# Two more load tiles that later hold the split weight parts, loads issued when their tile is free, and slices and list steps in another order

## The chip, the cores and the metric

The kernel runs on one core of a Trainium2 chip. The metric is the device time of one execution in microseconds (us). Before the change three runs took 1670.32, 1674.1 and 1680.08 us; the median is 1674.1.

## The reference: what is computed

One decoder layer on 1024 rows of 1024 columns (T = D = 1024), all in float32. Cut to what matters here:

```python
x = x + token_mixer(rmsnorm(x))          # ends with (g_a * y_a + g_b * y_b) @ w_o
h = rmsnorm(x)
# every row picks one of 4 groups, then two of the 8 experts in it
for each row t and each of its two experts e, with weight g:
    a, b = h[t] @ w_gate[e], h[t] @ w_up[e]         # 1024 -> 512
    out[t] += g * ((silu(a) * b) @ w_down[e])       # 512 -> 1024
x = x + out
x = x + sigmoid(rmsnorm(x) @ w_pg) * (p @ w_pp)
return rmsnorm(x)
```

There are 32 experts; the weights of one are 6 MB, so the experts' stage reads some 200 MB.

## The kernel before: how the work is staged and ordered

TensorE, ScalarE, VectorE and SP run their instructions in the order in which the program writes them from the w_o stage on. A wait of one instruction therefore holds all that is written behind it on its engine. GpSimd's order is left to the scheduler.

**The w_o stage** (818 to 962 us of the profile). There are eight tiles of 128 rows. A tile is 48 matmuls at L423, issued as ticks; `later` sets other work between the ticks of the next tile. When a tile's product is done, `rows_done` (L456) adds x, stores x2 (L502), and calls the functions in `on_rows`, which load weights for the experts. Then, in the ticks of the next tile: at tick 8 the transposes (L108) and `h2_store` (L513: VectorE computes h at L515 into the only h2 buffer, SP stores it at L516); at tick 18 the router's matmuls (L521) and `route_top`, which ends with the mask a at L550; at tick 33 `route_rank`, whose first matmul (L593) reads a, and which scatters two numbers per row into a table (L604). The last tile goes through `last_rows` (L470) instead.

**Weight tiles.** An expert's weights are six chunks of 1 MB (gate, up, gate, up, down, down). `load` (L664) issues one chunk on SP's queue into the next tile of the list `free`, and each load waits until the load five before it has landed. The list has 17 tiles of 8 KB per partition. The first is c0; a0 to a7 and b0 to b7 are tiles that hold the w_o stage's left operand M, so a load into one of them waits until TensorE has read it. `release` appends a tile to the list when its slot is done.

**The entry to the experts** (962 to 986 us). The last routing, the counts of rows per expert, the order of the experts in 32 slots, the index loads (L741 to L743), the first gathers (L701) and the copies of the transposed rows (L799).

**The experts' loop** (L1199, 986 to 1560 us). The string SLOTS gives each of the 32 slots a form: 32 rows (L), 64 (N), 64 + 32 (S), 128 (M), 128 + 32 (X), twice 128 (B), and one with twice 128, then 64, then 32 (A). A block of 128 rows is a wide block. For it the weights are split into a high and a low part so that three fast matmuls replace one (L843); narrow blocks multiply directly (L902, L929). The slots with wide blocks are 9 (B), 11 (X), 14 (M), 16 (A), 20 (B) and 25 (M), and each comes behind a narrow unit. A wide unit has 24 parts of 128x512: 16 for gate and up, 8 for down. A part is split by ScalarE (L97) and then by VectorE (L98), into one of four buffers (PARTS = 4, tiles wph and wpl). `Parts.get(n)` splits on until part n + 3 and hands out part n.

The loop runs one unit ahead: the second half of gate and up of unit u (k = 4 to 7), `act` (silu and product, L906 and L907), the first three k of unit u + 1, `hpose` (transposes and the copy at L916), the fourth k, the down products of u (L929), the stores of y (L940), the transposes of unit u + 2 (L797, L799). On some slots `p_step` adds work of the last stage (L1144). If an expert has more rows than its slot, the rest goes to an overflow list; its four steps on VectorE (`sizes`, L984 to L1023) were written in front of `start(u + 1)` at slots 20, 21, 22 and 23.

**The tail** (1560 to 1675 us) adds the experts' results and computes the last gate and norm.

Of the kernel before, what the change touches and what calls it, by code (L numbers as in the profile page):

```python
# [11 lines left out]
F32R = mybir.dt.float32r  # L12
# [11 lines left out]
NT = 8  # L24
# [14 lines left out]
AHEAD = 5  # L39
PASSES = ((0, 0), (0, 1), (1, 0))  # L40
PARTS = 4
SIZES = (20, 21, 22, 23)


A0, A1, A2, B1, B2, B3 = range(6)
# [14 lines left out]
UNITS = [(s, blocks) for s, k in enumerate(SLOTS) for blocks in KINDS[k]]  # L60
# [5 lines left out]
def layer_kernel(ctx: ExitStack, tc: tile.TileContext, A, out, dbg=None):  # L66
# [70 lines left out]
    big = ctx.enter_context(tc.tile_pool(name="big", bufs=1))  # L137
# [36 lines left out]
    with tc.tile_pool(name="s0", bufs=1, side="right") as s0:  # L174
# [5 lines left out]
        xs, first = [], []  # L180
        for tb in range(NT):
            if tb == 4:
                first = [wchunk(w_in, (4 - i) * D, load_only=True) for i in range(2)]
# [45 lines left out]
    with tc.tile_pool(name="s1", bufs=2) as s1:  # L229
        for cb in range(8):  # L230
# [4 lines left out]
            u = s1.tile([128, KB - 1 + T], F32, name="u")  # L235
# [174 lines left out]
    mpw = ctx.enter_context(tc.tile_pool(name="mpw", bufs=1))  # L410
# [23 lines left out]
    on_rows, last = {}, []  # L434
# [203 lines left out]
    tiles = {}  # L638

    def tile_of(name, dt=F32):  # L640

        if tiles.get(name, (None, None))[1] is not dt:
            tiles[name] = ((mpw if name[0] == "c" else big).tile([128, 2048], dt, name=name), dt)
        return tiles[name][0]

    XP = (mybir.EngineType.SP,)
    ORDER = list(range(6 * NE + 4))

    free = ["c0"] + [f"a{i}" for i in range(7)] + [f"b{i}" for i in range(8)] + ["a7"]
    held, loads = {}, []  # L650

    def chunk_src(c, e):
# [15 lines left out]
    def load(n=1, after=None, last=6 * NE):  # L668

        for _ in range(n):  # L670
            if not free or not ORDER or ORDER[0] >= last:
                return
            q = ORDER.pop(0)
            c, s = q % 6, q // 6
            if s not in ids:
                ids[s] = nc.values_load(slots[:, 1, s:s + 1], engines=XP, min_val=0, max_val=NE - 1)
            held[q] = free.pop(0)
            ld = load_raw(tile_of(held[q]), chunk_src(c, ids[s]), 4 if c < 4 and s < NE else 2)
            if after is None and len(loads) >= AHEAD:
                after = loads[-AHEAD]  # L680
            if after is not None:
                tc.add_manual_dep(ld.ins, after.ins.name,
                                  mybir.DependencyInfo(mybir.DependencyClass.Sync, mybir.DependencyReason.DATA),
                                  reason="few loads under way at once, for the gathers' sake")
                after = None
            loads.append(ld)
# [18 lines left out]
    n = []  # L705
# [10 lines left out]
    first = []  # L716


    for i in range(NT):
        on_rows[i] = [lambda i=i: load(0 if i == NT - 1 else 1 if i else 3)]  # L720

    def x_in(tb):
        if tb < NT:
# [47 lines left out]
    nb = mp.tile([1, 1, NE], F32, name="nb")  # L771
    cums = [mp.tile([1, NE], F32, name=f"cum{i}") for i in range(2)]
    mp.tile([128, 280], F32, name="padm")
    ysc, freeb, nxt = [], ["p0", "p1", "p2", "p3", "p4"], {"xg": 0, "y": 0, "hid": 0}

    def xtile(dt=F32):

# [2 lines left out]
    def turn(what):  # L780
        nxt[what] += 1
        return nxt[what] - 1
# [26 lines left out]
    class Parts:  # L809
# [8 lines left out]
            n -= 16  # L818
            return wpart(self.q + 4 + n // 4)[:, n // 2 % 2, n % 2 * 512:(n % 2 + 1) * 512]

        def get(self, n):
            while self.at < min(n + PARTS, 24):
                h, l = (mp.tile([128, 512], F32R, name=i, bufs=PARTS) for i in ("wph", "wpl"))
                split(h, l, self.raw(self.at))
                self.parts[self.at] = h, l
                self.at += 1
            return self.parts.pop(n)

    class Wide:
# [15 lines left out]
        def gate_up(self, k, j, w):  # L845
            self.mm(self.b[j], [self.x[:, a, k] for a in range(2)], w, k == 0, k == KT - 1)
# [128 lines left out]
    def sizes(step):  # L975

        if step in (1, 2):
            s = xtile()[0:1]
            le, eq = (s[:, i * NOV * NE:(i + 1) * NOV * NE].rearrange("p (i s) -> p i s", i=NOV) for i in range(2))
        (sizes0, sizes1, sizes2, sizes3)[step](*((le, eq) if step in (1, 2) else ()))  # L980
# [46 lines left out]
    def gathers(u):  # L1027

        if u >= len(UNITS):
            return  # L1030
        blocks[u] = []
        e, bs = UNITS[u]
        for r, b in bs:
            xg = XG[turn("xg") % 3]
            if u >= FIXED:
                if r < 128 and ROWS[e] == r:
                    by_few(r, on(n[e], E.Pool), lambda r: gather(xg[:r], places(e, r, b)))
                else:
                    gather(xg[:r], places(e, r, b))
            blocks[u].append([r, xg, None, places(e, r, b), 6 * e])  # L1040
# [18 lines left out]
    def start(u):  # L1059
        if u < len(UNITS):  # L1060
            for i, (r, xg, xt, ix, q) in enumerate(blocks[u]):
                blocks[u][i] = Wide(xt, ix, q) if r == 128 else Rows(r, *xt, ix, q)
            parts[u] = Parts(blocks[u][0].q)

    parts = {}

    def wide(u):
        return [b for b in blocks[u] if b.r == 128], [b for b in blocks[u] if b.r < 128]

    def gate_up(u, ks):  # L1070
        if u < len(UNITS):
            ws, ns = wide(u)
            for k in ks:
                for j in range(2 if ws else 0):
                    w = parts[u].get(2 * k + j)
                    for b in ws:
                        b.gate_up(k, j, w)
                for b in ns:
                    b.gate_up(k)

    def down(u):
        ws, ns = wide(u)
        for b in ns:
            b.down()
        for n in range(8 if ws else 0):
            w = parts[u].get(16 + n)
            for b in ws:
                b.down(n // 2, n % 2, w)

# [109 lines left out]
    for u, (e, _) in enumerate(UNITS):  # L1199
        first, last = (UNITS[u + i][0] != e if 0 <= u + i < len(UNITS) else True for i in (-1, 1))  # L1200
        if first and e + 4 < NE:
            sizes_load(e + 4)
        if first and e == NE - 4:
            nov = nc.values_load(ovi[0:1, 2 * NOV:], engines=(E.PE, E.Activation, E.DVE, E.SP), min_val=0, max_val=NOV)
        gathers(u + 3)
        if u:
            gate_up(u, range(4, 8))
        if last:
            for c in range(4):
                release(6 * e + c)  # L1210
            load(4)
        for b in blocks[u]:
            b.act()
        if first and e in SIZES:
            sizes(SIZES.index(e))
        start(u + 1)
        gate_up(u + 1, range(3))
        for i, b in enumerate(blocks[u]):
            b.hpose()
            if i == 0:  # L1220
                gate_up(u + 1, (3,))
        down(u)
        for b in blocks[u]:
            b.store()
        poses(u + 2)
        if last:
            release(6 * e + 4)
            release(6 * e + 5)
            p_step(e - PROJ)
            p_release(e - PROJ)  # L1230
            if e == NE - 3:
                tails = [tile_of("c2")]
                nc.sync.dma_start(x3_of(0), x2_dram[:128, :])
            load(6)
        if e == NE - 2:
            load(2, last=6 * NE + 4)
# [188 lines left out]
```

## Time and profile before

| | |
|---|---|
| profiled execution | 1677.25 us |
| its span, first to last instruction | 1675.5 us |
| mean granted clock of TensorE | 0.971 |
| TensorE busy | 1545.8 us (92%) |
| VectorE busy | 912.6 us (54%) |
| ScalarE busy | 448.1 us (27%) |
| GpSimd busy | 171.2 us (10%) |
| HBM traffic over the span | 202 GB/s |

The profile is one execution, so its rows belong to 1677.25 us and not to the median of 1674.1. A timeline row reads: start, duration, engine, line, operation, output<-inputs, shapes, count, and in brackets how long the engine was idle ahead of it and what ended that. In the names below PE is TensorE, DVE is VectorE, ACT is ScalarE, POOL is GpSimd, SP is SyncE; SPq rows are DMA issues.

### The profile page before, as it was taken

Reading aid. Unit: us, or ns where it says so; the run is one execution under the profiler, and the core shown is the slowest. Engines: PE = TensorE matmul, PEld = TensorE weight load, DVE = VectorE, ACT = ScalarE, POOL = GpSimd, SP = SyncE. Lnnn points to the kernel's source line nnn. Section 1 sums busy time; section 2 is a strip of 40 time slices with the busy share of each in tenths; the row PEclk is TensorE's granted clock in tenths of the full one; section 3 lists DMA queues with packets and bytes.
Section 4 is the critical chain, followed back from the end, with each engine's and each line's share of the span. In section 5 each row is a group of like instructions: output and inputs, shape, how many; then the busy total and the mean of one; then the engine's idle time right before and its main releaser. Section 6 shows DMA issues by size and latency. Waiting matters only on the chain. (4 is left out here: it accounts for less than half of the span.)

```text
span 1675.5 us, 21390 instructions
## 1 busy us (share of the span) xinstructions
PE 1545.8 (92%) x8328; PEld 1116.4 (67%) x8328; DVE 912.6 (54%) x1266; ACT 448.1 (27%) x695; POOL 171.2 (10%) x318
## 2 busy tenths in 40 slices
PE   6999999999999999999988758999999897889798
PEld 4888888888888888888766623346466462443586
DVE  4899999999972523514533322135463343331575
ACT  4222121112211314622411101024353230220443
POOL 2300000000000001000011111111111101110131
PEclk9999999999999999999999969999999998998999
DMA  5222112211144523444444679999995997899741
GB/s 167 61 64 63 47 54 63 63 55 51 59 142 135 162 89 125 139 138 151 154 173 128 234 279 364 407 409 407 399 405 206 378 369 284 320 372 412 297 164 51
DMA packets 190674, 336.81 MB, mean 201 GB/s; under 512 B 10182, under 2 KB 85022, under 8 KB 190560
## 3 DMA queue, kind: packets, MB, share of 16 engines
q1 hardware_dynamic: 174080, 284.13, 47.1%
q0 software_dynamic: 10576, 29.96, 4.9%
q10 hardware_dynamic: 5904, 21.24, 3.9%
q8 instruction: 67, 1.10, 0.3%
q14 instruction: 47, 0.39, 0.1%
HBM read 302.67 MB, written 35.11 MB: 202 GB/s over the span
## 5 line engine op out<-in xcount | busy, mean ns | idle before, releaser
L164 PE MATMUL mm<-a,wh 128*128 128x512 f32 x1792 | 555.9, 391 | 0.9 <-ACT a L215 0.9
L164 PEld LDWEIGHTS mm<-a,wh 128*128 128x128 f32 x1792 | 336.9, 188 | 70.9 <-ACT a L215 1.5
L164 PE MATMUL mm<-a,wl 128*128 128x512 f32 x896 | 349.3, 390 | 0.0
L256 DVE SCALAR_TENSOR_TENSOR acc<-u,cw,acc 128x1024 f32<-128x1024 f32 x240 | 307.9, 1283 | 7.9 <-ACT acc L239 1.9
L97 ACT ACTIVATE wh<-wraw 128x1024 fp32r<-128x1024 f32 x72 | 76.4, 1061 | 494.7 <-PE mm L164 423.1
L164 PEld LDWEIGHTS mm<-a,wl 128*128 128x128 f32 x896 | 168.5, 188 | 34.7
L164 PE MATMUL mm<-b,wh 128*128 128x512 f32 x512 | 157.5, 389 | 0.0
L843 PE MATMUL p<-wph,xt 128*128 128x512 f32 x432 | 145.1, 405 | 9.3 <-ACT wph L97 9.1
L98 DVE TENSOR_TENSOR wl<-wraw,wh 128x1024 fp32r<-128x1024 f32 x72 | 87.7, 1219 | 72.6 <-ACT wh L97 72.5
L902 PE MATMUL p<-b,xt 128*32 128x256 f32 (+1 forms) x896 | 117.6, 451 | 3.6 <-DMA b<-in_w_exp_up_dram 3.4
L164 PEld LDWEIGHTS mm<-b,wh 128*128 128x128 f32 x512 | 96.1, 188 | 20.0
L843 PEld LDWEIGHTS p<-wph,xt 128*128 128x128 f32 x432 | 82.0, 191 | 37.4 <-ACT wph L97 13.6
L423 PE MATMUL mm<-b,a 128*128 128x512 f32 x384 | 100.6, 412 | 1.4 <-DVE b L98 1.3
L164 PE MATMUL mm<-b,wl 128*128 128x512 f32 x256 | 99.6, 389 | 0.0
L902 PE MATMUL p<-a,xt 128*32 128x256 f32 (+1 forms) x624 | 93.8, 467 | 6.2 <-DMA a<-in_w_exp_gate_dram 3.8
L843 PE MATMUL p<-wpl,xt 128*128 128x512 f32 x216 | 86.1, 399 | 2.1 <-DVE wpl L98 2.1
L940 DVE COPY ys<-p 32x256 f32<-32x256 f32 (+1 forms) x51 | 25.0, 491 | 115.1 <-ACT ys L940 114.7
L423 PEld LDWEIGHTS mm<-b,a 128*128 128x128 f32 x384 | 72.3, 195 | 17.3 <-DVE b L98 2.6
L902 PEld LDWEIGHTS p<-b,xt 128*32 128x32 f32 (+1 forms) x896 | 36.3, 118 | 65.3 <-issue 47.5
L98 DVE TENSOR_TENSOR wpl<-a,wph 128x512 fp32r<-128x512 f32 x88 | 58.9, 687 | 29.1 <-ACT wph L97 28.8
L940 ACT COPY ys<-p 32x256 f32<-32x256 f32 (+1 forms) x51 | 21.3, 417 | 188.5 <-PE p L929 175.7
L97 ACT ACTIVATE wph<-a 128x512 fp32r<-128x512 f32 x88 | 54.5, 629 | 40.6 <-PE p L843 18.8
(333 smaller groups left out, 1667.0 us busy)
## 6 DMA issues: line engine op xcount, KB each, us to landing
a<-in_w_exp_up_dram SPq DMA_DIRECT2D x31, 1024.0 KB, 12.7
a<-in_w_exp_down_dram SPq DMA_DIRECT2D x31, 1024.0 KB, 13.6
b<-in_w_exp_gate_dram SPq DMA_DIRECT2D x30, 1024.0 KB, 15.3
b<-in_w_exp_down_dram SPq DMA_DIRECT2D x30, 1024.0 KB, 13.0
b<-in_w_exp_up_dram SPq DMA_DIRECT2D x29, 1024.0 KB, 12.6
wraw<-in_w_in_dram SPq DMA_DIRECT2D x56, 512.0 KB, 3.7
a<-in_w_exp_gate_dram SPq DMA_DIRECT2D x28, 1024.0 KB, 12.5
ut<-u_dram ACTq DMA_DIRECT2D x24, 512.0 KB, 4.0
```

Of the source, the lines that this page charges most:

```text
L97: nc.scalar.activation(h, src, AF.Copy)
L98: nc.vector.tensor_tensor(l, src, h.bitcast(F32), op=OP.subtract)
L164: nc.tensor.matmul(ps[:, hf], w[wi][:, k], act[ai][k][:, hf * 512:(hf + 1) * 512], start=(k == 0 and i == 0), stop=(k == KT - 1 and i == 2))
L256: nc.vector.scalar_tensor_tensor(acc, u[:, t:t + T], cw[:, cb, t:t + 1], acc, op0=OP.mult, op1=OP.add)
L423: nc.tensor.matmul(ps[-1][:, hf], act(a, k), w(b, k)[:, hf * 512:(hf + 1) * 512], start=(k == 0 and i == 0), stop=(k == nk - 1 and i == 2))
L843: nc.tensor.matmul(o, x[a], w[b], start=first and i == 0, stop=last and i == 2)
L902: nc.tensor.matmul(self.gu[j][p:p + r], self.x[:, k], w[:, i:i + self.gu[0].shape[1]], start=(k == 0), stop=(k == KT - 1))
L940: (nc.scalar.copy if c < len(self.d) // 2 else nc.vector.tensor_copy)(self.y[:, c * n:(c + 1) * n], d)
```

## The change

1. The list of free tiles gets two more, d0 and d1, behind c0. They take loads until chunk 42 (RETIRE, the first of slot 7); from there on they leave the list. The parts of the wide units are then slices of them: four slices of 512 columns of d0 hold the high parts, four of d1 the low ones. The buffers wph and wpl, of the same size together, are gone.
2. `rows_done` of the first tile loads four chunks in place of three, so each later tile's load takes the M tile that has just been multiplied, in place of the next one.
3. `start(u + 1)` stands ahead of the second half of unit u, and where u is narrow and u + 1 wide, `ahead` splits four parts there. `gate_up` gets a limit on how far parts are split: 7 in the first three k, 9 in the fourth.
4. The four steps of the overflow list stand behind `hpose`, at slots 18, 19, 21 and 22.

```diff
-SIZES = (20, 21, 22, 23)
+RETIRE = 42
+SIZES = (18, 19, 21, 22)
...
-            tiles[name] = ((mpw if name[0] == "c" else big).tile([128, 2048], dt, name=name), dt)
+            tiles[name] = ((mpw if name[0] in "cd" else big).tile([128, 2048], dt, name=name), dt)
...
-    free = ["c0"] + [f"a{i}" for i in range(7)] + [f"b{i}" for i in range(8)] + ["a7"]
+    free = ["c0", "d0", "d1"] + [f"a{i}" for i in range(7)] + [f"b{i}" for i in range(8)] + ["a7"]
...
         for _ in range(n):
+            if free and ORDER and free[0][0] == "d" and ORDER[0] >= RETIRE:
+                free.pop(0)
...
-        on_rows[i] = [lambda i=i: load(0 if i == NT - 1 else 1 if i else 3)]
+        on_rows[i] = [lambda i=i: load(0 if i == NT - 1 else 1 if i else 4)]
...
-        def get(self, n):
-            while self.at < min(n + PARTS, 24):
-                h, l = (mp.tile([128, 512], F32R, name=i, bufs=PARTS) for i in ("wph", "wpl"))
+        def ahead(self, n):
+            while self.at < min(n, 24):
+                i = turn("part") % PARTS
+                h, l = (tile_of(t, F32R)[:, i * 512:(i + 1) * 512] for t in ("d0", "d1"))
                 split(h, l, self.raw(self.at))
                 self.parts[self.at] = h, l
                 self.at += 1
+
+        def get(self, n, limit):
+            self.ahead(min(n + PARTS, limit))
             return self.parts.pop(n)
...
+    def ahead(u, n):
+        if u < len(UNITS) and wide(u)[0]:
+            parts[u].ahead(n)
+
-    def gate_up(u, ks):
+    def gate_up(u, ks, limit=24):
...
-                    w = parts[u].get(2 * k + j)
+                    w = parts[u].get(2 * k + j, limit)
...
         gathers(u + 3)
+        start(u + 1)
+        if blocks[u][0].r < 128:
+            ahead(u + 1, PARTS)
         if u:
             gate_up(u, range(4, 8))
...
-        if first and e in SIZES:
-            sizes(SIZES.index(e))
-        start(u + 1)
-        gate_up(u + 1, range(3))
+        gate_up(u + 1, range(3), 7)
         for i, b in enumerate(blocks[u]):
             b.hpose()
             if i == 0:
-                gate_up(u + 1, (3,))
+                gate_up(u + 1, (3,), 9)
+        if first and e in SIZES:
+            sizes(SIZES.index(e))
         down(u)
```

Three places of the instruction order show it. The first is SP's queue in the w_o stage, from the end of the first tile's product on; numbers tell the tiles of a name apart, a0 to a2 are M tiles, x2 and h2 are the rows and their norm. Before:

```order
L502 DMA x2_dram_66<-x2_5279 128x1024
L664 DMA c0_5341<-in_w_exp_gate_dram 128x4x512
L664 DMA a0_5343<-in_w_exp_up_dram 128x4x512
L664 DMA a1_5345<-in_w_exp_gate_dram 128x4x512
L725 DMA x2_5347<-in_x_dram 128x1024
L516 DMA h2_dram_67<-h2_5369 128x1024
L502 DMA x2_dram_66<-x2_5281 128x1024
L664 DMA a2_5483<-in_w_exp_up_dram 128x4x512
L725 DMA x2_5485<-in_x_dram 128x1024
L516 DMA h2_dram_67<-h2_5507 128x1024
```

And now:

```order
L504 DMA x2_dram_66<-x2_5279 128x1024
L666 DMA c0_5341<-in_w_exp_gate_dram 128x4x512
L666 DMA d0_5343<-in_w_exp_up_dram 128x4x512
L666 DMA d1_5345<-in_w_exp_gate_dram 128x4x512
L666 DMA a0_5347<-in_w_exp_up_dram 128x4x512
L729 DMA x2_5349<-in_x_dram 128x1024
L518 DMA h2_dram_67<-h2_5371 128x1024
L504 DMA x2_dram_66<-x2_5281 128x1024
L666 DMA a1_5485<-in_w_exp_down_dram 128x2x1024
L729 DMA x2_5487<-in_x_dram 128x1024
L518 DMA h2_dram_67<-h2_5509 128x1024
```

Ahead of the first store of h the last load went into a1, which the second tile still reads; it now goes into a0, which the first tile has read. The same holds one tile further on (a2 before, a1 now).

The second place is VectorE between slot 10 (narrow) and slot 11 (wide and narrow): L98, now L100, is the split of a part, L907, now L915, slot 10's product, L916, now L924, the copy that its down product reads, L940, now L948, its store. Before:

```order
L907 TENSOR_TENSOR hid_6444<-p_7823,hid_6444 64x256
L98 TENSOR_TENSOR wpl<-b_6454,wph 128x512
L98 TENSOR_TENSOR wpl<-a_6456,wph 128x512
...
L98 TENSOR_TENSOR wpl<-c_5341,wph 128x512
L916 COPY xt<-h 128x128
L98 TENSOR_TENSOR wpl<-a_5343,wph 128x512
L98 TENSOR_TENSOR wpl<-c_5341,wph 128x512
L960 UNCONDITIONAL_BRANCH
L940 COPY ys<-p_8108 32x256 x2
L799 COPY xt<-x_8141 128x512
L960 UNCONDITIONAL_BRANCH
L98 TENSOR_TENSOR wpl<-a_5343,wph 128x512
```

And now:

```order
L100 TENSOR_TENSOR d_7550<-b_6286,d_7549 128x512
L915 TENSOR_TENSOR hid_6446<-p_7703,hid_6446 64x256
L100 TENSOR_TENSOR d_7550<-b_6249,d_7549 128x512
L100 TENSOR_TENSOR d_7550<-b_6286,d_7549 128x512
L100 TENSOR_TENSOR d_7550<-b_6249,d_7549 128x512
L924 COPY xt<-h 128x128
L100 TENSOR_TENSOR d_7550<-b_6286,d_7549 128x512
L100 TENSOR_TENSOR d_7550<-b_6346,d_7549 128x512
L968 UNCONDITIONAL_BRANCH
L948 COPY ys<-p_8038 32x256 x2
L803 COPY xt<-x_8071 128x512
```

Four splits have moved ahead of slot 10's product; three stand between the product and the copy, where nine stood, and two between the copy and the store of y, as before, so that nine of the 24 parts are split ahead of that store in place of eleven.

The third place is GpSimd at the entry to the experts: L604, now L606, is a scatter of the last tile's routing, L701, now L705, the first gather of rows. Before:

```order
L489 TENSOR_TENSOR rs<-rs,mhalf 128x1
L604 DMA table<-pay,dst 32768x2 x2
L701 DMA c_5276<-h_dram,idx_82 64x1024
L708 TENSOR_LOAD slots
L708 ISA x2
```

And now:

```order
L491 TENSOR_TENSOR rs<-rs,mhalf 128x1
L705 DMA c_5276<-h_dram,idx_82 64x1024
L606 DMA table<-pay,dst 32768x2 x2
L712 TENSOR_LOAD slots
L712 ISA x2
```

The gather now stands ahead of the last two scatters.

More of the change, by code (lines that the diff above doesn't have):

```diff
@@ L773, in layer_kernel @@
     mp.tile([128, 280], F32, name="padm")
-    ysc, freeb, nxt = [], ["p0", "p1", "p2", "p3", "p4"], {"xg": 0, "y": 0, "hid": 0}
+    ysc, freeb, nxt = [], ["p0", "p1", "p2", "p3", "p4"], {"xg": 0, "y": 0, "hid": 0, "part": 0}
     def xtile(dt=F32):
@@ L1085, in down @@
         for n in range(8 if ws else 0):
-            w = parts[u].get(16 + n)
+            w = parts[u].get(16 + n, 24)
             for b in ws:
```

## The prediction

> **What bounds the kernel now.** I read the page's slices first, then the list of waits, then the timelines of the stages that the change touches. Each digit of the slices is a tenth of 41.9 us.
>
> ```profile
> PE   6999999999999999999988758999999897889798
> DMA  5222112211144523444444679999995997899741
> ```
>
> TensorE is busy nearly everywhere, so a gain has to come from stretches in which it waits. The low slices 21 to 24 are the w_o stage and the entry to the experts; from slice 25 on transfers are near their limit as well. The waits, with total, count and longest one, show a ring of three in the w_o stage:
>
> ```profile
> PE tp L593 <- DVE a L550: 25.4, 7, 4.8
> DVE h L515 <- DMA h_dram<-h: 49.9, 6, 9.5
> SPq L664 <- PE mm L423: 102.6, 9, 18.3
> ```
>
> Read from below: SP stands 102.6 us at a weight load whose tile is still being multiplied; the store of h queued behind it is late; VectorE cannot overwrite the one h buffer (49.9 us); the routing behind that is late, and TensorE waits for its mask a (25.4 us). SP and VectorE rows of the first two tiles show one turn:
>
> ```profile
> 847.42 0.37 SPq L664 DMA_DIRECT2D a<-in_w_exp_gate_dram  x1
> ...
> 848.44 0.37 SPq L516 DMA_DIRECT2D h_dram<-h  x1
> ```
>
> ```profile
> 836.73 1.28 DVE L515 SCALAR_TENSOR_TENSOR h<-x,rs,gf 128x1024 f32<-128x1024 f32 x1 [2.25 <-POOL rs L103]
> ...
> 856.72 1.28 DVE L515 SCALAR_TENSOR_TENSOR h<-x,rs,gf 128x1024 f32<-128x1024 f32 x1 [8.07 <-DMA h_dram<-h]
> ```
>
> h of tile 0 is ready at 836.73 + 1.28 = 838.0, its store goes out 10.4 us later, right behind the load at 847.42, and VectorE waits 8.07 us for it.
>
> **Term 1, the w_o loads.** TensorE's rows there (start, duration, what it waited for):
>
> ```profile
> 834.54 1.09 PE L108 MATMUL tp<-ident,x 128*128 128x128 f32 x8 [0.67 <-DVE x L458]
> ...
> 848.83 1.04 PE L108 MATMUL tp<-ident,x 128*128 128x128 f32 x8
> ...
> 879.15 3.73 PE L423 MATMUL mm<-b,a 128*128 128x512 f32 x9
> ...
> 915.38 2.29 PE L423 MATMUL mm<-b,a 128*128 128x512 f32 x9
> ...
> 934.57 3.77 PE L423 MATMUL mm<-b,a 128*128 128x512 f32 x9
> ...
> 941.78 1.04 PE L108 MATMUL tp<-ident,x 128*128 128x128 f32 x8
> ...
> 967.99 0.18 PE L593 MATMUL tp<-a,tri 128*128 128x32 bf16 x1 [3.60 <-DVE a L550]
> ```
>
> A tile whose predecessor's store is not yet needed takes 848.83 - 834.54 = 14.29 us; the next five take 941.78 - 848.83 = 92.95 instead of 71.45, that is 21.5 too many. Of the 25.4 us of waits the last, 3.60, is the last tile's own routing with no matmuls left to cover it; it stays. The other six make 21.8. Two of them left the clock at half for nine matmuls (3.73 and 3.77 against 2.29): 2.9 more. Every load now takes a tile that is free when it is issued, so the store goes out when h is ready. Removed: 21.8 + 2.9 = 24.7. What comes late next: four loads stand together behind row 0. At 2.6 us each (term 3) they and 1.5 MB of x, x2 and h, ahead of or behind them, need some 14 us from 835, so h of tile 0 lands at about 850 to 851; VectorE wants the buffer at 836.73 + 14.29 = 851.0, and later tiles have one load each in 14.29 us. I take **-25**, with ends -28 and -21.
>
> **Term 2, the entry to the experts.** GpSimd's rows, and ScalarE's that TensorE's first expert matmul waits for:
>
> ```profile
> 970.39 1.04 POOL L604 DMA_INDIRECT table<-pay,dst  x1 [6.47 <-DVE sm L557]
> 971.74 0.96 POOL L604 DMA_INDIRECT table<-pay,dst  x1 [0.30 <-issue]
> 973.00 1.02 POOL L701 DMA_INDIRECT c<-h_dram,idx  x1 [0.30 <-issue]
> ```
>
> ```profile
> 984.45 0.59 ACT L799 COPY xt<-x 128x512 f32<-128x512 f32 x1 [12.17 <-DMA x_dram<-x]
> ```
>
> The first gather now stands ahead of the last two scatters. SP's next load, and the index loads and the x2 store behind it, wait for that gather, which starts 973.00 - 970.39 = 2.6 us earlier; the index loads also need the scatters, which start 1.3 us later. Between -2.6 and +1.3; I take **-1**.
>
> **Term 3, two more chunks loaded ahead.** Waits of TensorE for weights in the first slots, the rate of the full stretch, and SP later on:
>
> ```profile
> 1026.40 1.09 PE L902 MATMUL p<-b,xt 128*64 128x512 f32 x1 [2.49 <-DMA b<-in_w_exp_up_dram]
> ...
> 1044.18 4.80 PE L902 MATMUL p<-b,xt 128*64 128x512 f32 x34 [0.90 <-DMA b<-in_w_exp_up_dram]
> ```
>
> ```profile
> 1100.00:1200.00 100.00, 93.11 (x596) 57.34 (x596) 50.46 (x83) 42.06 (x74) 13.39 (x14) 1.00 1.04 407
> ```
>
> ```profile
> 1261.24 33.00 SPq L664 DMA_DIRECT2D b<-in_w_exp_down_dram  x2
> ```
>
> At 407 GB/s (last column) a chunk of 1.05 MB takes 2.6 us, so two chunks are a lead of some 5 us: more than the 2.49 + 0.90 = 3.4 us waited. I take **-3.4** (0 to -5). At 1261 SP's two loads span 33 us, as it waits for a free tile: by there transfers have run ahead of the work, and dropping the two tiles at slot 7 costs no supply.
>
> **Term 4, parts split ahead.** From the page's groups (busy, mean ns, idle before, releaser) and around slot 20:
>
> ```profile
> L843 PE MATMUL p<-wph,xt 128*128 128x512 f32 x432 | 145.1, 405 | 9.3 <-ACT wph L97 9.1
> ...
> L843 PE MATMUL p<-wpl,xt 128*128 128x512 f32 x216 | 86.1, 399 | 2.1 <-DVE wpl L98 2.1
> ```
>
> ```profile
> 1331.21 0.50 PE L843 MATMUL p<-wph,xt 128*128 128x512 f32 x1 [1.56 <-ACT wph L97]
> ...
> 1333.91 0.50 PE L843 MATMUL p<-wph,xt 128*128 128x512 f32 x1 [0.56 <-ACT wph L97]
> ```
>
> ```profile
> 1333.22 2.19 ACT L97 ACTIVATE wph<-a 128x512 fp32r<-128x512 f32 x4 [2.07 <-DMA a<-in_w_exp_up_dram]
> ```
>
> The 11.4 us stand at the six starts of wide units, where TensorE arrives before the first parts are split. With four parts split before the narrow unit's second half, they are ready. Not so at slot 20: there ScalarE itself waits 2.07 us for the chunk, so 1.56 + 0.56 = 2.1 remain. **-9.3** (-5 to -12).
>
> **Term 5, fewer parts ready in second halves.** Only part 8 is now ready when a wide unit goes on, where 8, 9 and 10 were; part 9's split stands behind the stores of y and the copy of the next x. Slot 11, and the price of a split:
>
> ```profile
> 1175.63 0.50 PE L843 MATMUL p<-wph,xt 128*128 128x512 f32 x1
> ```
>
> ```profile
> 1175.92 0.85 DVE L940 COPY ys<-p 32x256 f32<-32x256 f32 x2 [2.45 <-ACT ys L940]
> 1176.80 0.69 DVE L799 COPY xt<-x 128x512 f32<-128x512 f32 x1
> ```
>
> ```profile
> L98 DVE TENSOR_TENSOR wpl<-a,wph 128x512 fp32r<-128x512 f32 x88 | 58.9, 687 | 29.1 <-ACT wph L97 28.8
> ...
> L97 ACT ACTIVATE wph<-a 128x512 fp32r<-128x512 f32 x88 | 54.5, 629 | 40.6 <-PE p L843 18.8
> ```
>
> Part 8 feeds three matmuls of 0.4 us, until 1176.8; VectorE is free of the copy at 1177.5 and has part 9 at 1178.2: a new wait of 1.4. Six units like it would cost 8.4; units with two blocks have twice the matmuls as cover and 0.2 left over. I take 1.4 for slot 11, 2.4 for the three other units with one wide block and 0.5 for the two with two: **+4.3** (0 to +9).
>
> **Term 6, the overflow list's steps.** Waits at slots 21 and 22, and the same work undisturbed:
>
> ```profile
> 1396.53 3.68 PE L929 MATMUL p<-b,xt 128*64 128x512 f32 x8 [4.11 <-DVE xt L916]
> ...
> 1404.75 5.40 PE L1144 MATMUL x<-b,b 128*128 128x512 f32 x8 [1.30 <-DVE xt L799]
> ...
> 1418.96 3.61 PE L929 MATMUL p<-a,xt 128*32 128x256 f32 x32 [4.82 <-DVE xt L916]
> ...
> 1440.75 3.70 PE L1144 MATMUL x<-b,b 128*128 128x512 f32 x8 [1.51 <-DVE xt L98]
> ```
>
> ```profile
> 1050.88 3.65 PE L929 MATMUL p<-b,xt 128*64 128x512 f32 x16
> ...
> 1189.81 1.93 PE L929 MATMUL p<-a,xt 128*32 128x256 f32 x32 [0.38 <-DVE xt L916]
> ```
>
> VectorE does a list step of four to six us ahead of the copy that the down product needs; behind that copy the steps run beside the product (3.65 us) and only its end, some 1.1 us each at slots 19 and 21, delays the y stores and the next copies. So -4.11 - 4.82 + 2.2 = -6.7. The clock was at half after these waits: the second product took 3.61 instead of 1.93, and eight matmuls of the first took 3.68, as long as sixteen undisturbed ones (3.65). I take -1.7 - 1.8. **-10.2** (-5 to -14). The matmuls of the projection at 1404.75 also ran at half (5.40 against 3.70), after a wait of only 1.30; as that wait stays, I return nothing for them.
> [...]
>
> **The sum.** -25 - 1 - 3.4 - 9.3 + 4.3 - 10.2 = -44.6. The profiled execution took 1677.25 us, 1675.5 of them span; minus 44.6 that is 1632.65. It lies 3.15 above the median of the three runs, 1674.1, which gives 1629.5. As two small gains are left out (half clock in the last tile and at slot 14, for which I have quoted no row), I say **1628**. About 0.5%, 8.4 us, is what a measurement of this kernel can tell from no change.
>
> **The rivals.** A, *transfers are the bound* from the experts' entry on: terms 4 to 6 give nothing, as TensorE then waits for weights instead. 1674.1 - 29.4 = 1644.7. For it: the 407 GB/s. Against it: SP's long wait for a tile at 1261 and TensorE's 93% in that window. Chance 0.09.
> B, *the four loads hold the queue*: h's store lies behind 4 MB on SP's queue; if it is late by the 10 us of those loads and each later load is again ahead of its store, term 1 goes: 1628 + 25 = 1653. Against it: 851 and 851.0 meet in tile 1, and later tiles have 2.6 us of load per 14.29. Chance 0.08.
> [...] No run here shows four loads ahead of a store.
> C, *slower*: the four parts are slices of two tiles. Were every split to wait for all readers of its tile, each of 6 x 24 = 144 parts would show its 0.63 + 0.69 = 1.32 us, 190 us in all: 1818. It decides from 44.6 / 144 = 0.31 us a part. Against it: y's halves are slices of one tile too, and copies into one go on beside a scatter of the other; the wait in 1175.92 is for ScalarE alone. Chance 0.03.
> D, *nothing moves*: the loads still wait for matmuls, as new free tiles only shift names, and the rest cancels: 1674. Against it: the order of loads shown with the change names tiles already read. Chance 0.03.
>
> **How the numbers follow.** My forecast has 0.77. Its terms' ends, not all at once, make 1612 to 1648, and A lies inside: 0.77 x 0.92 + 0.09 is about 0.8. Faster by over 0.5% are forecast, A and B: 0.94; within it D: 0.03; slower C: 0.03.
>
> **What would show it.** Right: no wait of SP's loads for matmuls of L423, one wait of about 3.6 left at the rank matmul, tiles of 14.3 us, no waits of 4 us at the down products, short new waits at part 9. Wrong: waits for h's store remaining (B), waits for weights at wide starts (A), a split per 1.3 us with TensorE idle (C).

## The result, and the profile after

The changed kernel took 1631.77 us, the median of four runs (1628.60 to 1638.78), beside 1675.49 us for the kernel before: a ratio of 0.9746, with a 95% interval of 0.970 to 0.979. Beside the experiments, in two more sittings that the record puts on one chip, the ratio was 0.968 (0.9655 to 0.9706) and 0.974 (0.9714 to 0.977). These two intervals do not touch, so ratios of different sittings can differ by 0.6% with nothing changed. The forecast was 1628 in a range of 1612 to 1648, with a chance of 0.94 for faster. The profiled execution took 1638.78 us, its span is 1637.0: 38.5 us less than the profiled one before, where the sum said 44.6. It was the slowest of its four; the two later traces of the same kernel, on the chip of those sittings, have spans of 1631.0 and 1632.4, 44.5 and 43.1 us less.

The slices of the page after, to be set against the two rows of before:

```profile
PE   6999999999999999999989968999999888988898
DMA  5221122112225443534385689999996989999641
```

There is one low slice at the entry to the experts now, number 24, and the ones of the w_o stage are filled. The list of waits, with the ring of three in it:

```profile
PE tp L595 <- DVE a L552: 5.8, 2, 3.6
...
DVE h L517 <- DMA h_dram<-h: 6.8, 1, 6.8
...
SPq L666 <- PE mm L425: 4.3, 3, 3.7
```

SP's 102.6 us at the loads are 4.3, VectorE's 49.9 us for the h buffer are one wait of 6.8, and TensorE's 25.4 us are 5.8 in two waits. TensorE's rows show where the two are:

```profile
849.46 1.04 PE L110 MATMUL tp<-ident,x 128*128 128x128 f32 x8
...
860.15 0.19 PE L595 MATMUL tp<-a,tri 128*128 128x32 bf16 x1 [2.16 <-DVE a L552]
...
865.99 1.03 PE L110 MATMUL tp<-ident,x 128*128 128x128 f32 x8
...
874.37 0.19 PE L595 MATMUL tp<-a,tri 128*128 128x32 bf16 x1
...
880.19 1.04 PE L110 MATMUL tp<-ident,x 128*128 128x128 f32 x8
...
922.89 1.04 PE L110 MATMUL tp<-ident,x 128*128 128x128 f32 x8
...
943.66 0.18 PE L595 MATMUL tp<-a,tri 128*128 128x32 bf16 x1 [3.60 <-DVE a L552]
```

From 865.99 on a tile takes 14.2 us (865.99 to 880.19, and 56.90 for the four up to 922.89). Only the second tile, behind the burst of four loads, waited 2.16 us, and the last kept its 3.60.

Both traces have 8328 matmuls in the same order, so the start of one matmul in the trace after can be set against its start before. How far the changed kernel is ahead shows term by term where the time came from:

| TensorE's instruction | before | after | after less before | term, and its step |
|---|---|---|---|---|
| transposes behind w_o tile 0 | 834.54 | 835.17 | +0.63 | |
| last tile's rank matmul | 967.99 | 943.66 | -24.33 | 1: -25.0 |
| first expert matmul | 985.09 | 958.48 | -26.61 | 2: -2.3 |
| slot 6's down product | 1050.88 | 1022.61 | -28.27 | 3: -1.7 |
| start of slot 20 (B) | 1331.21 | 1301.14 | -30.07 | 4 and 5: -1.8 |
| transposes in slot 20 | 1350.55 | 1325.12 | -25.43 | 6: +4.6 |
| slot 21's down product | 1396.53 | 1366.78 | -29.75 | 6: -4.3 |
| slot 22's down product | 1418.96 | 1382.94 | -36.02 | 6: -6.3 |
| a projection step | 1440.75 | 1403.03 | -37.72 | 6: -1.7 |
| start of slot 25 (M) | 1449.28 | 1410.24 | -39.04 | 4: -1.3 |
| end of the span | 1675.5 | 1637.0 | -38.5 | |

The two later traces give -25.7 and -25.5 for the first step, -2.5 and -2.1 for the second, -3.5 and -3.2 for the third and -4.4 and -2.2 for the fourth, so a step of a few us in one trace is good to some two us.

One row is of the wrong sign: behind slot 19 the changed kernel loses 4.6 us. TensorE before:

```profile
1350.55 1.84 PE L108 MATMUL x<-ident,a 128*128 128x128 f32 x8 [1.49 <-DVE xt L799]
```

And after, with VectorE ahead of it:

```profile
1318.61 0.70 PE L801 MATMUL x<-ident,xg 64*128 64x64 f32 x8
1325.12 1.97 PE L110 MATMUL x<-ident,b 128*128 128x128 f32 x8 [5.80 <-DVE xt L803]
```

```profile
1312.19 0.42 DVE L924 COPY xt<-h 128x256 f32<-128x256 f32 x1 [3.11 <-PE h L923]
...
1318.73 1.15 DVE L1009 TENSOR_TENSOR xt<-cum,iota_s 1x960 f32<-1x960 f32 x1 [4.91 <-PE p L937]
...
1323.65 0.69 DVE L948 COPY ys<-p 64x512 f32<-64x512 f32 x1
1324.37 0.69 DVE L803 COPY xt<-x 128x512 f32<-128x512 f32 x1
```

The list step (L1009 and four more up to 1323.6) should have run beside the down product, from 1313.8 on, when VectorE was free. It waited 4.91 us until that product (L937) had ended, and so all its length stood ahead of the store of y and of the copy that TensorE needs next.

### The profile page after: what moved, and what is told of

Same layout as the page of the kernel before. It is cut to its first block, busy times and chain, and to the rows that moved or that the text cites. A ratio compares the mean times of both kernels' runs of the same rounds, so it can differ in the third digit from the quotient of the medians.

```text
span 1637.0 us, 21380 instructions
## 1 busy us (share of the span) xinstructions
PE 1534.2 (94%) x8328; PEld 1109.7 (68%) x8328; DVE 911.4 (56%) x1266; ACT 446.3 (27%) x695; POOL 172.1 (11%) x318
## 5 line engine op out<-in xcount | busy, mean ns | idle before, releaser
L851 PE MATMUL p<-d,xt 128*128 128x512 f32 x648 | 163.7, 404 | 8.7 <-ACT d L99 4.4
L851 PEld LDWEIGHTS p<-d,xt 128*128 128x128 f32 x648 | 120.1, 191 | 48.3 <-DVE d L100 8.0
L100 DVE TENSOR_TENSOR wl<-wraw,wh 128x1024 fp32r<-128x1024 f32 x72 | 87.8, 1220 | 73.0 <-ACT wh L99 72.8
L910 PE MATMUL p<-a,xt 128*32 128x256 f32 (+1 forms) x824 | 113.7, 447 | 4.9 <-DMA a<-in_w_exp_gate_dram 4.2
L425 PE MATMUL mm<-b,a 128*128 128x512 f32 x384 | 96.0, 399 | 1.3 <-DVE b L100 1.3
L910 PE MATMUL p<-b,xt 128*32 128x256 f32 (+1 forms) x616 | 90.9, 465 | 4.4 <-DMA b<-in_w_exp_up_dram 4.2
L948 DVE COPY ys<-p 32x256 f32<-32x256 f32 (+1 forms) x51 | 25.0, 491 | 102.7 <-ACT ys L948 102.2
L948 ACT COPY ys<-p 32x256 f32<-32x256 f32 (+1 forms) x51 | 21.3, 418 | 190.0 <-PE p L937 177.8
L910 PEld LDWEIGHTS p<-a,xt 128*32 128x32 f32 (+1 forms) x824 | 36.3, 117 | 50.4 <-issue 37.2
L100 DVE TENSOR_TENSOR d<-b,d 128x512 fp32r<-128x512 f32 x76 | 50.1, 687 | 23.8 <-ACT d L99 23.7
L789 POOL DMA_INDIRECT y_dram<-ys,idx x39 | 37.1, 951 | 195.7 <-DVE ys L875 55.7
L910 PEld LDWEIGHTS p<-b,xt 128*32 128x32 f32 (+1 forms) x616 | 25.6, 119 | 45.7 <-issue 35.6
```

Source lines behind the costliest of these rows:

```text
L100: nc.vector.tensor_tensor(l, src, h.bitcast(F32), op=OP.subtract)
L425: nc.tensor.matmul(ps[-1][:, hf], act(a, k), w(b, k)[:, hf * 512:(hf + 1) * 512], start=(k == 0 and i == 0), stop=(k == nk - 1 and i == 2))
L789: st = nc.gpsimd.indirect_dma_start(out=y_dram, out_offset=bass.IndirectOffsetOnAxis(ap=ix[:, 1:2], axis=0), in_=y, in_offset=None, bounds ...
L851: nc.tensor.matmul(o, x[a], w[b], start=first and i == 0, stop=last and i == 2)
L910: nc.tensor.matmul(self.gu[j][p:p + r], self.x[:, k], w[:, i:i + self.gu[0].shape[1]], start=(k == 0), stop=(k == KT - 1))
L948: (nc.scalar.copy if c < len(self.d) // 2 else nc.vector.tensor_copy)(self.y[:, c * n:(c + 1) * n], d)
```

## The experiments

The theory to be tested: the gain is the ring of waits in the w_o stage first and the list steps second; the parts add little; the list step at slot 19 loses time because of its place. The rivals are named with each run. Ratios are to the kernel before on the same chip in the same sitting. There were three sittings. Loads alone, Three loads, Steps earlier and the first Parts undone ran in the first, without the unedited changed kernel, so their distance from it is not measured. No limits, Steps in front and the first of Both small mends ran in the second, the second Parts undone and the last run in the third, each beside the changed kernel.

**Loads alone.** The kernel before, with two loads behind the first tile in place of three. No tile is added; each later load takes a tile already read.

```diff
-        on_rows[i] = [lambda i=i: load(0 if i == NT - 1 else 1 if i else 3)]
+        on_rows[i] = [lambda i=i: load(0 if i == NT - 1 else 1 if i else 2)]
```

> The kernel before, with one edit: two loads behind the first tile of the w_o stage instead of three, so that each later load takes a tile already read. My theory, that the first term of the sum stands by itself: the w_o stage (848.83 to 954 in the profile before) becomes 22 to 26 us shorter, one wait of about 3.6 us for the mask stays, and no wait appears in the second tile either, since only two loads stand ahead of the first store of h. One chunk fewer is loaded ahead, worth 2.5 us in the first slots. Time 19 to 25 us below the kernel before. Rival, that transfers are the bound behind it: the stage is as much shorter, but the experts' loop waits that much longer for weights, and the time falls by under 10 us.

Measured: 1649.86 us beside 1684.29, 34.4 us less, a ratio of 0.9796 (0.9763 to 0.983); that is more than the 19 to 25 us expected. The profiled execution took 1650.97, 26.3 below the one before, which is of another sitting; the difference of 8 us between the two figures is open. TensorE's rows:

```profile
847.57 1.03 PE L108 MATMUL tp<-ident,x 128*128 128x128 f32 x8
855.96 0.19 PE L593 MATMUL tp<-a,tri 128*128 128x32 bf16 x1
861.78 1.04 PE L108 MATMUL tp<-ident,x 128*128 128x128 f32 x8
...
939.49 0.19 PE L593 MATMUL tp<-a,tri 128*128 128x32 bf16 x1 [3.61 <-DVE a L550]
```

The last rank matmul comes at 939.49 in place of 967.99, 28.5 us earlier; 1.2 of that stand ahead of the stage, so the stage is 27.3 us shorter (22 to 26 were expected). The second tile does not wait. GpSimd's first gather stands ahead of the last two scatters in this run too (941.35 against 942.72), so it also has what the prediction called term 2. The lead is 31.4 us at the first expert matmul; 7.1 of it go by the start of slot 20, most of them at the starts of wide units, where the waits for ScalarE are 11.6 us in place of 9.1, and 26.3 are left at the end. One digit gives more than half of the whole change; the rival, that transfers take it back, falls.

**Three loads.** The changed kernel with a burst of three.

```diff
-        on_rows[i] = [lambda i=i: load(0 if i == NT - 1 else 1 if i else 4)]
+        on_rows[i] = [lambda i=i: load(0 if i == NT - 1 else 1 if i else 3)]
```

> The changed kernel with three loads behind the first tile of the w_o stage instead of four. Theory of the queue: the first store of h lies behind four loads and lands late, which costs 2.2 us in the second tile; with three it lands 2.5 us earlier, the wait of 6.8 us for it becomes about 4 and TensorE's 2.2 us go to 0; one chunk fewer is loaded ahead, so waits for weights in the first slots grow by up to 2.5. Within 2 us of the changed kernel in all. Rival, that the wait has another cause (SP's own 3.1 us at the load of x behind them): the 2.2 us stay.

Measured: 1632.75 us, ratio 0.9677 (0.9642 to 0.9712). VectorE's and TensorE's rows in the second tile:

```profile
854.02 1.28 DVE L517 SCALAR_TENSOR_TENSOR h<-x,rs,gf 128x1024 f32<-128x1024 f32 x1 [4.59 <-DMA h_dram<-h]
```

```profile
858.08 0.19 PE L595 MATMUL tp<-a,tri 128*128 128x32 bf16 x1
```

The wait for the store falls from 6.83 to 4.59 us and TensorE's 2.16 us go, as the theory said. But SP's long issue went too: the load of x took it 0.73 us in place of 3.13, so TensorE's wait alone does not tell the theory from the rival. The landing of the store says more. SP issued it 2.85 us earlier (838.85 against 841.70), and yet the buffer came free only 2.1 us earlier (854.02 against 856.11). This is the stretch from the first load of the burst to the landing, first with four loads and then with three; the last two numbers of a row are the busy share of the DMA engines and GB/s:

```profile
835.63:855.97 20.34, 20.34 (x115) 17.14 (x114) 6.85 (x32) 5.58 (x12) 3.73 (x6) 1.00 1.02 335
```

```profile
835.80:853.90 18.10, 18.10 (x103) 15.14 (x101) 6.85 (x32) 5.58 (x12) 3.74 (x6) 1.00 0.97 313
```

The DMA engines are all but fully busy in both (1.02 and 0.97). That the store waits for the transfers of the burst ahead of it is the author's reading of these figures; no run has four loads and a short issue, which would show it directly. The fourth chunk gives something in exchange: TensorE's waits for weights in the first slots are 3.2 us here, and 2.5, 1.8 and 1.1 in three traces of the changed kernel.

**Parts undone.** The changed kernel with the third edit taken back, run twice.

```diff
-        start(u + 1)
-        if blocks[u][0].r < 128:
-            ahead(u + 1, PARTS)
...
-        gate_up(u + 1, range(3), 7)
+        start(u + 1)
+        gate_up(u + 1, range(3))
...
-                gate_up(u + 1, (3,), 9)
+                gate_up(u + 1, (3,))
```

> The changed kernel with its third edit undone: the next unit's start back behind the act, no parts split ahead, no limits. My theory: 7 to 9 us of waits at wide starts come back (1.0 to 2.4 each at slots 9, 11, 14, 16 and 25), and 2 to 3 us of new waits at part 9 in second halves go, so 4 to 7 us slower than the changed kernel. Rival, that these waits only trade places with waits for weights: within 2 us of the changed kernel.

> The third edit undone, a second time, now with the changed kernel on the same chip. My theory, from the first trace, in which TensorE ends 4.1 us behind the changed kernel's: 3 to 6 us slower than the changed kernel. Rival, that the waits only trade places: within 2 us.

Measured: 1639.87 us, 0.9728 (0.970 to 0.9757) the first time; the second time 1632.26 us, 0.9752 (0.9728 to 0.9775), beside the unedited changed kernel on the same chip:

> The changed kernel, unedited, beside the two others on one chip: ratio to the kernel before 0.966 to 0.976.

which took 1632.16 us, 0.9742 (0.9714 to 0.977). The two medians differ by 0.1 us: this theory of 3 to 6 us fell, and the rival held. The waits at the parts show why the gain is small; first with the parts undone, then the changed kernel on that chip:

```profile
PE p L851 <- ACT d L99: 6.9, 6, 1.2
...
PE p L851 <- DVE d L100: 2.1, 7, 0.5
```

```profile
PE p L851 <- DVE d L100: 4.3, 7, 1.2
...
PE p L851 <- ACT d L99: 2.7, 3, 1.3
```

Splitting ahead takes 4.2 us off the waits for ScalarE (6.9 to 2.7); the second halves give 2.2 back (2.1 to 4.3). This is one pair of traces: all waits at the parts are 12.0 and 9.0 us in the two traces with the parts undone, and 8.4, 5.3 and 7.0 in three of the changed kernel. So some 2 to 5 us of waits go; why the medians show none of it is open. And 1.3 of the 2.7 stand at slot 14, where the parts split ahead come no earlier than before, as ScalarE's rows of the changed kernel show:

```profile
1177.52 0.58 ACT L948 COPY ys<-p 64x512 f32<-64x512 f32 x1 [7.52 <-DMA y_dram<-ys,idx]
1178.00 1.07 ACT L99 ACTIVATE xt<-x 128x512 fp32r<-128x512 f32 x2
1178.96 2.19 ACT L99 ACTIVATE d<-b 128x512 fp32r<-128x512 f32 x4
```

The four splits (1178.96) stand behind the store of y (1177.52), which waits 7.52 us for an earlier scatter out of ys.

**No limits.** The changed kernel with the parts split ahead, but without 7 and 9.

```diff
-        gate_up(u + 1, range(3), 7)
+        gate_up(u + 1, range(3))
...
-                gate_up(u + 1, (3,), 9)
+                gate_up(u + 1, (3,))
```

> The changed kernel without the limits of 7 and 9 on the parts split early, the four parts split ahead kept. My theory: parts 9 and 10 are ready again when a wide unit goes on, so the new waits at part 9 (1.2 at slot 11, 0.9 at slot 14, 0.6 at slot 16) go, and nothing comes back, as the ring of four holds the splits back anyway: 2 to 3 us faster than the changed kernel, by the trace. Rival, that the limits keep splits out of the way of the narrow unit's copy for its down product: the short waits at part 9 go, but waits of 0.5 to 1.5 us appear at the down products or at their copies, and the time stays the same or is slower by up to 4 us.

> The changed kernel itself, unedited, so that the three kernels beside it can be set against it on one chip. Ratio to the kernel before as measured at first, 0.97 to 0.98.

Measured: 1627.24 us, 0.9664 (0.9639 to 0.9689), beside 1628.85 us, 0.968 (0.9655 to 0.9706), for the changed kernel on that chip (0.97 to 0.98 was expected of it). The intervals overlap, and the span is 1.2 us shorter, where 2 to 3 were expected. The waits at the parts, without limits:

```profile
PE p L851 <- ACT d L99: 2.1, 1, 2.1
...
PE p L851 <- DVE xt L100: 0.7, 1, 0.7
...
PE p L937 <- DVE xt L924: 0.4, 1, 0.4
PE p L851 <- DVE d L100: 0.2, 1, 0.2
```

The waits for VectorE's splits fall from 4.3 to 0.9 us, those for ScalarE's rise from 1.0 to 2.1, and at the down products nothing is added (0.4, as in the changed kernel). The limits protect nothing that this trace shows. Where the time went can be seen in the trace: set matmul against matmul, it goes from 2.0 us behind the changed kernel's in the w_o stage (863.32 against 861.31) to 3.5 ahead in front of slot 20 (1287.88 against 1291.40), and 2.1 of that go at slot 20's start (1298.26 against 1299.72), where the one wait of 2.1 is for a part whose weights come late.

**Steps in front.** The fourth edit undone: list steps ahead of the next unit's first half, at slots 20 to 23.

```diff
-SIZES = (18, 19, 21, 22)
+SIZES = (20, 21, 22, 23)
...
-        gate_up(u + 1, range(3), 7)
+        if first and e in SIZES:
+            sizes(SIZES.index(e))
+        gate_up(u + 1, range(3), 7)
...
-        if first and e in SIZES:
-            sizes(SIZES.index(e))
         down(u)
```

> The changed kernel with its fourth edit undone: list steps in front of the next unit's first half, at slots 20 to 23. My theory: waits of 4.1 and 4.8 us come back at the down products of slots 21 and 22, with the half clock behind them, 10 to 11 us; the 5.8 us at the projection's transposes behind slot 19 shrinks to 1.5 (4.3 us), and two waits of 1.1 more at the projection's products shrink. Net 5 to 7 us slower than the changed kernel. Rival, that the net of this edit is near zero, since what the product saves the stores lose: within 2 us.

Measured: 1638.13 us, 0.9739 (0.9716 to 0.9763), 9.3 us above the changed kernel's 1628.85, where 5 to 7 were expected. The waits:

```profile
PE p L937 <- DVE xt L924: 9.3, 3, 4.8
...
PE x L110 <- DVE xt L803: 1.5, 1, 1.5
```

The 9.3 us at the down products are back, and the 5.8 behind slot 19 is 1.5. By the traces the end moves by 5 to 7 us, by the medians by 9.3; the sign and the two places are as expected.

**Steps earlier.** The first two steps one slot earlier, nothing else.

```diff
-SIZES = (18, 19, 21, 22)
+SIZES = (17, 18, 21, 22)
```

> The changed kernel with the first two list steps at slots 17 and 18 instead of 18 and 19. My theory: at slot 19 the step finds all three buffers for transposed rows taken (slot 20 has two wide blocks), takes the one of slot 19 itself and so begins only when the down product has ended; one slot earlier there is a free buffer, the step begins beside the product, and the 5.8 us wait at the projection's transposes becomes 1.5 or less; what it delays at slot 18 goes into the wait for weights at slot 20's start. 3 to 5 us faster than the changed kernel. Rival, that the place of the step does not matter, only its 4.8 us on VectorE: the wait moves to slot 18 and the time stays within 1 us.

Measured: 1625.33 us, 0.9655 (0.9628 to 0.9681); the 3 to 5 us against the changed kernel can be read from traces alone. VectorE at slot 18, and TensorE at the transposes that waited 5.80 us:

```profile
1277.22 0.29 DVE L924 COPY xt<-h 128x128 f32<-128x128 f32 x1 [2.78 <-PE h L923]
1277.43 1.13 DVE L1009 TENSOR_TENSOR xt<-cum,iota_s 1x960 f32<-1x960 f32 x1
```

```profile
1283.95 1.71 PE L810 MATMUL x<-ident,c 128*128 128x128 f32 x8 [2.87 <-DVE xt L100]
...
1310.79 1.09 PE L110 MATMUL x<-ident,b 128*128 128x128 f32 x8 [1.49 <-DVE xt L803]
```

The same step now begins right behind its copy, without the 4.91 us, and the wait is 1.49. Against the kernel before, the way from the start of slot 20 to these transposes is 4.1 to 4.6 us longer in three traces of the changed kernel, and 1.8 shorter here (1.0 and 1.1 shorter in the two runs below, which have the same edit). So the place of the step matters, and the rival falls. At slot 18 a wait of 1.5 grows to 2.87, ahead of the start of slot 20, where ScalarE waits for weights in every trace (1.70 to 2.51 us for its chunk of up, 2.51 here). The program has three buffers named xt, and slot 20 needs two of them; that the step at slot 19 had to take slot 19's own is read from the wait for L937, and the step's freedom at slot 18 agrees with it. A fourth buffer was not tried.

**Both small mends.** First three loads with the earlier steps, then four loads, the earlier steps and no limits.

```diff
-SIZES = (18, 19, 21, 22)
+SIZES = (17, 18, 21, 22)
...
-        on_rows[i] = [lambda i=i: load(0 if i == NT - 1 else 1 if i else 4)]
+        on_rows[i] = [lambda i=i: load(0 if i == NT - 1 else 1 if i else 3)]
```

> The changed kernel with three loads behind the first tile and list steps at slots 17, 18, 21 and 22. My theory: both places add up, 2 us in the second tile of the w_o stage less up to 2.5 of lead, and 4 to 5 us behind slot 19: 4 to 7 us faster than the changed kernel. Rival, that waits for weights take these back: within 2 us of it.

Measured: 1625.29 us, 0.9654 (0.963 to 0.9678), 3.6 us below the changed kernel on that chip, between theory and rival. Its trace is 1.3 us ahead of the changed kernel's in the w_o stage (858.04 against 859.34) and 5.0 behind it in front of slot 20 (1291.82 against 1286.78), 2.9 us of it in waits for weights in the first slots (4.7 us in place of 1.8), the rest without a shown cause; the transposes in slot 20 then give 5.1 back.

```diff
-SIZES = (18, 19, 21, 22)
+SIZES = (17, 18, 21, 22)
...
-        gate_up(u + 1, range(3), 7)
+        gate_up(u + 1, range(3))
...
-                gate_up(u + 1, (3,), 9)
+                gate_up(u + 1, (3,))
```

> The changed kernel with four loads as it is, list steps at slots 17, 18, 21 and 22, and no limits on the parts. My theory: 4 to 5 us behind slot 19 and 2 us in second halves add up, 5 to 7 us faster than the changed kernel. Rival, that the wait for weights at slot 20's start grows by what comes before it: 4 us or less.

Measured: 1620.53 us, 0.9664 (0.9639 to 0.969), 11.6 us below the changed kernel on that chip (1632.16; the intervals do not touch). All that is left of waits at the parts is

```profile
PE p L851 <- DVE d L100: 0.9, 2, 0.7
```

This is the lowest median of the study, though by ratio two runs above, of other sittings, are as low (0.9655 and 0.9654). It gains more than the 5 to 7 us expected. Its trace is 1.8 us behind the changed kernel's at the first expert and 7.4 ahead at 1228, where only the limits differ, then 6.5 ahead at the start of slot 20 and 12.4 behind its transposes. The 9.2 us of the first stretch are more than the 5.5 that the limits gave alone; 2.3 of them come up to 1048, ahead of the first wide unit, where the edits have nothing to act on, and for the rest the cause is open.

## Why the prediction was right, point by point

The medians moved by 43.7 us, where the sum had 44.6. The mechanism of the largest term and the places of the others were right; that the total is so close is in part luck, as term 2 gave more than its size and term 6 less.

**Term 1** (-25): measured -25.0. The ring was the cause, and the edit of one digit shows it alone. That it came out to the tenth is luck: a new wait of 2.2 us was not in the term, and neither were 2.4 us that came back beside it, 1.5 of them the last tile's matmuls, which take 3.80 us ahead of the last seven in place of 5.31, at a granted clock of 1.00 in place of 0.68, and which the sum had kept out of its terms. What the prediction weighed as rival B did happen, in one tile: 850 to 851 against 851.0 was too close, h's store went out 841.70 and the buffer came free at 856.1. The step that failed there is the time of h's landing, short by 5 us: the sum had 5.7 MB at 407 GB/s in 14 us, and the trace has 6.8 MB at 335 GB/s in 20.3 us. SP's 3.13 us at the load of x do not explain it: with three loads, where SP took 0.73 us, such a sum gives 11.5 us and the trace has 18.1. The cost was 2.2 us (1.6 in each of the two later traces), and it was a matter of one tile, as said, since later tiles have one load each.

**Term 2** (-1, ends -2.6 and +1.3): -2.3. **Term 3** (-3.4, ends 0 and -5): -1.7 up to slot 6, and -3.5 and -3.2 in the two later traces. The step "more than the 2.49 + 0.90 = 3.4 us waited" failed: TensorE's waits for weights in the first slots go from 4.1 us (0.7, 2.5 and 0.9) to 2.5, 1.8 and 1.1 in the three traces, so a lead of 5 us does not end them. What else holds those weights back was not tried, and no run takes the two new tiles away by themselves. The longer waits for weights, 5.0 us before and 8.0, 4.7 and 5.7 after, stand near the end of the loop (from 1468 on in the trace after), where the term promised nothing.

**Terms 4 and 5** (-9.3 and +4.3, together -5.0): -3.1 in the table, and -5.7 and -3.5 in the two later traces. The waits at the parts before are 11.2 us by their releasers, not quite the 11.4 of the prediction. The sum left 2.1 + 4.3 = 6.4 us of them; there are 8.4 in the first trace after (4.4 for ScalarE, 4.0 for VectorE), and 5.3 and 7.0 in the later ones. The new waits of term 5, at part 9, are 1.2, 0.9, 0.6 and 0.5 us at slots 11, 14, 16 and 25, 3.2 in all where the term had 4.3: it counted four units with one wide block, and there are three. Of term 4, the step that failed in two of the three traces is "With four parts split before the narrow unit's second half, they are ready": it looked at what is written behind the splits and not at what stands ahead of them on ScalarE. At slot 14 that is a store of y held by a scatter. And the edit's own share is smaller than the waits: without it they are 12.0 and 9.0 us, with the other edits in, and the medians with and without it are equal within their intervals.

**Term 6** (-10.2): -7.7. The two waits at the down products went, as the sum had it, and more came back of the half clock than it had taken: some 4.4 us in place of 3.5, as the first product took 6.3 us and takes 3.65, and the second 3.61 and 1.9. Against that, the wait at the projection of slot 21 grew by 1.4 us, where 1.1 was allowed for, and behind slot 19 4.6 us came where 1.1 was allowed for. The step that failed is "behind that copy the steps run beside the product": a step needs a scratch buffer too, and at slot 19 the only one was held by the very product beside which it was to run. At slot 21 the step did start beside the product (1366.64 against 1366.78).

On the clock, the projection's eight matmuls at slot 21 still take 5.39 us, with a granted clock of 0.50 from 1373.72 to 1377.13, behind a wait that grew from 1.30 to 2.68 us, with no wait of 4 us ahead of them any more:

```profile
1366.78 3.65 PE L937 MATMUL p<-b,xt 128*64 128x512 f32 x16
1370.36 0.68 PE L801 MATMUL x<-ident,c 32*128 32x32 f32 x8
1373.72 5.39 PE L1156 MATMUL x<-b,a 128*128 128x512 f32 x8 [2.68 <-DVE xt L803]
```

The two down products ran at full speed again (3.65 us for the sixteen matmuls of the first), as the sum had it. The prediction returned nothing for the half clock at 1404.75, behind a wait of 1.30 us; whether it was left over from the wait of 4.11 us ahead of that is seen in the kernel before. Here are three stretches around those matmuls, with TensorE's busy time, the granted clock, the busy share of the DMA engines and GB/s:

```profile
1395.10:1401.93 6.83, 5.40 (x14) 0.50 0.37 120
1401.93:1405.34 3.41, 2.11 (x14) 1.00 0.99 342
1405.34:1408.76 3.42, 3.42 (x6) 0.50 1.05 378
```

The clock was full again from 1401.93 to 1405.34, with TensorE busy for 2.11 of those 3.41 us, and then fell to 0.50 a second time, behind the wait of 1.30 us. So the half clock at 1404.75 was not left over from the wait of 4.11 us, and the prediction was right to return nothing for it.

**The rivals.** A, transfers as the bound, did not hold as a whole. ScalarE waits for weights at the start of slot 20 in every trace (1.70 to 2.51 us), and without limits 2.1 of the 3.5 us gained ahead of it went there. It is no firm bound: the last run comes there earliest of all, and TensorE's longest wait at that start is 0.2 us. B held for one tile. C did not hold: all waits at the 144 parts sum to 5.3 to 8.4 us, not 190. D fell with the first step of the table.

## What to carry to other kernels

In the kernel before, a load on SP's queue at 847.42 had waited for its tile, and the store of h written behind it went out at 848.44, 10.4 us after h was ready: ask of each load in such a queue whether its destination is free at the moment of issue, and shift the order of destinations before buying more of them; here one digit was worth 26 us by the traces and 34 by the medians of one sitting. When a step is moved beside other work, check what it waits for in its own buffers, and what is written ahead of it on its engine, not only what it delays. Gains of a few us ahead of a place that waits for transfers need not add up: one run kept 1.4 of 3.5 us, and another came to more than the sum of its parts, so measure them together.

## What the runs showed of the hardware

The clock fell to 0.50 behind a wait of 2.68 us with 0.68 us of short transposes ahead of it (above), while a wait of 2.16 us in the middle of dense matmuls left it at full speed, nine matmuls in 2.34 us. In the same place of the kernel before, waits of 2.96, 2.97 and 3.40 us left it at full speed too (nine in 2.29 us), and waits of 3.93 and 4.82 us did not (3.73 and 3.77 us). The row behind the wait of 2.16 us:

```profile
860.21 2.34 PE L425 MATMUL mm<-b,a 128*128 128x512 f32 x9
```

Issuing a DMA can hold SP itself: 3.13 us for one issue behind four loads of 1 MB, where the median of its 355 issues is 0.37 us. With three loads the same issue took 0.73 us.

```profile
837.69 0.72 SPq L666 DMA_DIRECT2D a<-in_w_exp_up_dram  x1
838.46 3.13 SPq L729 DMA_DIRECT2D x<-in_x_dram  x1
841.70 1.17 SPq L518 DMA_DIRECT2D h_dram<-h  x1
```
